# Delta-rule layer of a hybrid decoder trunk: small-tile products of a head pair gathered outside its chunk loop

## Chip, cores and metric

The kernel runs on one core of one Trainium2 chip. The metric is the time of one execution on the device, in microseconds (us); lower is better.

## What is computed

Four decoder layers run one after another over 1024 tokens of 1024 channels: a short gated convolution, a state-space layer, a delta-rule layer (RWKV-7 time mixing), and a second convolution layer. After each mixer come a gated projection and a layer norm. The change lies in the delta-rule layer alone. Per head of 64 channels it keeps a 64 by 64 state and walks over the tokens:

```python
def _rwkv_step(state, inp):
    r_t, w_t, k_t, v_t, kk_t, a_t = inp
    sa = jnp.einsum("bhvk,bhk->bhv", state, -kk_t)
    state = (state * w_t[:, :, None, :] + sa[..., None] * (kk_t * a_t)[:, :, None, :]
             + v_t[..., None] * k_t[:, :, None, :])
    out = jnp.einsum("bhvk,bhk->bhv", state, r_t)
    return state, out
```

The kernel does this by chunks of 64 tokens. Within a chunk the corrections of the tokens depend on each other through a triangular matrix, so a chunk needs the inverse of a unit triangular 64 by 64 matrix; then the state goes from chunk to chunk. Decay w, rate a, keys k, values v, queries r and the gate z come from projections of the shifted input. The outputs are group-normed, get a bonus, and are gated by silu(z).

## The kernel before, in words

The wide projections (`mm3`, lines 299 to 313) take three products of 128 by 128 by 512 per block of 128 input channels, with each operand split in a high and a low part. Their weights are loaded and split ahead by `wload` (line 277).

`rwkv_layer` (line 1289) goes over two halves of 512 tokens. Per half it first computes two low-rank products for decay and rate (`lora`, line 1314): 16 products into one accumulator `pwa` (lines 1329 to 1334), each fed by a freshly built mix. Then come eight blocks of the gate z (`use_z`), which also make the decay and rate of a block out of the low-rank results with a high-part product over 128 rows and a low-part product over 64 rows (lines 1360 to 1365). Then eight blocks of v (`use_v`). Last comes the phase of keys and queries, one head pair (a block m of 128 channels, two heads, eight chunks; pairs are numbered 0 to 7) after another:

- `use_k` (line 1393) makes keys and correction queries. Line 1408 sums squares, line 1419 takes the reciprocal, and lines 1422 to 1427 spread it over the channels with eight products of a broadcast column against the identity (16 passes on TensorE; every product of plain 32-bit numbers in this kernel shows as two passes, a transpose as one). Lines 1436 to 1438 transpose the queries.
- `use_r` (line 1443) makes the queries and the bonus.
- `prep` (line 1649) makes the scores of the pair's chunks (line 1672), copies out the diagonal 32 by 32 blocks, transposes the keys (line 1696), and forms the values' share of the correction (line 1707) with the two halves of the array (chunk parity w) in turns.
- `tsolve` (line 1714) inverts the diagonal blocks on VectorE.
- `join` (line 1747) puts the diagonal inverses together into the inverse T of each 64 by 64 matrix: for each parity w first the products zp (line 1765), a copy, the products tp (line 1770), a copy. Then the corrected queries a2 (line 1781). All these are products of 32 or 64 rows and columns.
- `seq` (line 1788) walks the eight chunks. Per chunk: the state product p1 (line 1801, 128 by 128), the inverse times the values added to it (line 1804, two products of 64 by 64), a copy to `uv` on ScalarE (line 1805), the key product p2 in two halves of 64 columns (line 1809), two updates of the state on VectorE (line 1812), the output products in two halves added to p1 (line 1816), a copy of the output (line 1817). After the loop: group norm, bonus, gate, and a store of the block (lines 1819 to 1850).

The eight banks of PSUM in this layer are three for the wide products (`pmm`), two in `paux` (preparation, join, `use_z`, `use_v`), one in `pk` (`pwa`, and the small products of `use_k` and `use_r`), and two in `pseq`, where p1, p2 and the transpose of the output take turns.

The functions are generators, and `rwkv_layer` (lines 1512 to 1575) pulls them in turns: `seq` of pair m-2 and `tsolve` of pair m-1 beside `use_k` and `use_r` of pair m; then `prep` of pair m, the join of pair m-1, and so on. The steps of `seq` and `tsolve` are issued with a raised priority (`PS, PT = 300, 300`, by `prio`, line 1463); a planner puts the instructions of each engine in a fixed order before the kernel runs, by these priorities and by what depends on what. Each engine then works through its list in that order. A buffer that is asked for again is given in program order, when its earlier tenant has been read.

## Time and profile before

| What | Value |
|---|---|
| median of three runs | 2888.84 us |
| lowest and highest of them | 2883.97 and 2890.22 us |
| span of the profiled execution | 2887.0 us |
| TensorE products, weight loads | 2790.6 us (97%), 2193.9 us (76%) |
| VectorE, ScalarE, GpSimd | 1916.1 us (66%), 1137.6 us (39%), 641.8 us (22%) |

The span runs from the first to the last instruction of one profiled execution. The profiled execution's whole time is not listed apart from the three runs; its span lies between the lowest and the highest of them. PE is TensorE's products, PEld its weight loads, DVE is VectorE, ACT ScalarE, POOL GpSimd. PEclk is the clock that TensorE was granted, as a share of full speed. Busy times of PE are modelled from overlapping products: the distance from one start to the next says more than the duration.

### The profile page before, as it was taken

To read this page: it belongs to the slowest core of one execution; us is meant where nothing else is said; L and a number is where in the kernel's file an instruction comes from. 1 tells how busy PE (TensorE), PEld (TensorE's weight loads), DVE (VectorE), ACT (ScalarE), POOL (GpSimd) and SP (SyncE) were. 2 spreads that over 40 slices of the span, in tenths; PEclk is the share of its full clock that TensorE was granted. 3 is DMA by queue.
4 is the path that set the end of the run, shared out by engine and by line. 5 is a ranking of instruction groups with operands and counts; after the bars stand their busy time and mean duration, and the time that the engine had idled before them with its cause. 6 is when DMAs were issued, how large, how long until landed. Compare 5 with 4: busy or idle time off the path is not lost. (4 is left out here: it accounts for less than half of the span.)

```text
span 2887.0 us, 41522 instructions
## 1 busy us (share of the span) xinstructions
PE 2790.6 (97%) x15515; PEld 2193.9 (76%) x15515; DVE 1916.1 (66%) x3428; ACT 1137.6 (39%) x2229; POOL 641.8 (22%) x689
## 2 busy tenths in 40 slices
PE   8999999999999999999999899999999999999998
PEld 7887788778877887677676577777778778888887
DVE  6777765476657348877987776898757473333654
ACT  3333322232254224665555665565434231112322
POOL 1243413221107043003333102333132210000000
PEclk9999999999999999997998899999899999999999
DMA  5333322267773234452222254222334332112311
GB/s 166 98 96 94 95 75 66 89 177 208 223 243 108 94 100 131 153 181 84 91 76 86 84 174 140 73 80 74 99 105 141 101 88 59 51 44 66 117 65 38
DMA packets 449752, 312.72 MB, mean 108 GB/s; under 512 B 48360, under 2 KB 393744, under 8 KB 449552
## 3 DMA queue, kind: packets, MB, share of 16 engines
q1 hardware_dynamic: 449552, 310.08, 35.6%
q8 instruction: 122, 2.00, 0.3%
q14 instruction: 78, 0.64, 0.1%
HBM read 240.28 MB, written 69.21 MB: 107 GB/s over the span
## 5 line engine op out<-in xcount | busy, mean ns | idle before, releaser
L286 DVE TENSOR_TENSOR wl<-wraw,wh 128x1024 fp32r<-128x1024 f32 x283 | 367.1, 1298 | 305.6 <-ACT wh L285 301.2
L285 ACT CAST wh<-wraw 128x1024 fp32r<-128x1024 f32 x283 | 297.3, 1051 | 687.9 <-PE gp L309 185.6
L1812 DVE SCALAR_TENSOR_TENSOR state<-state,pc,p 64x64 f32<-64x64 f32 x256 | 71.5, 279 | 79.0 <-PE p L1809 70.9
L608 POOL TENSOR_TENSOR ln_s<-ln_s,rp 128x512 f32<-128x512 f32 x42 | 61.5, 1464 | 204.9 <-DVE rp L604 204.9
L1738 DVE TENSOR_TENSOR tv<-ti,mi 128x128 f32<-128x128 f32 (+3 forms) x128 | 91.7, 716 | 3.2 <-PE tp L1770 1.1
L1805 ACT COPY uv<-p 64x128 f32<-64x128 f32 x128 | 33.4, 261 | 126.5 <-PE p L1804 125.2
L308 PE MATMUL zp<-x_0h,wh 128*128 128x512 f32 x192 | 76.8, 400 | 0.0
L310 PE MATMUL gp<-r_0h,wl 128*128 128x512 f32 x192 | 76.4, 398 | 0.0
L308 PE MATMUL gp<-r_1h,wh 128*128 128x512 f32 x192 | 76.3, 398 | 0.0
L310 PE MATMUL gp<-r_1h,wl 128*128 128x512 f32 x192 | 76.2, 397 | 0.2 <-DVE wl L286 0.2
L623 POOL TENSOR_TENSOR rp<-r_0h,r_0l 128x512 f32<-128x512 f32 x24 | 39.9, 1690 | 163.9 <-PE op L309 163.9
L308 PE MATMUL zp<-x_1h,wh 128*128 128x512 f32 x192 | 75.8, 395 | 0.0
L308 PE MATMUL gp<-r_0h,wh 128*128 128x512 f32 x192 | 75.8, 395 | 0.0
L310 PE MATMUL zp<-x_1h,wl 128*128 128x512 f32 x192 | 75.8, 395 | 0.0
L309 PE MATMUL gp<-r_0l,wh 128*128 128x512 f32 x192 | 75.8, 395 | 0.0
L309 PE MATMUL zp<-x_0l,wh 128*128 128x512 f32 x192 | 75.7, 394 | 0.0
L309 PE MATMUL zp<-x_1l,wh 128*128 128x512 f32 x192 | 75.7, 394 | 0.0
L310 PE MATMUL zp<-x_0h,wl 128*128 128x512 f32 x192 | 75.7, 394 | 0.0
L309 PE MATMUL gp<-r_1l,wh 128*128 128x512 f32 x192 | 75.4, 393 | 0.0
L1672 PE MATMUL s<-ra,kb 64*128 64x128 f32 x512 | 71.5, 320 | 1.1 <-DVE ra L1444 1.1
L1816 PEld LDWEIGHTS p<-uv,scr 128*64 128x64 f32 x512 | 43.2, 145 | 37.9 <-ACT uv L1805 22.7
L1801 PEld LDWEIGHTS p<-state,ra 128*128 128x128 f32 x256 | 46.3, 205 | 29.5 <-issue 7.5
(738 smaller groups left out, 8626.5 us busy)
## 6 DMA issues: line engine op xcount, KB each, us to landing
wraw<-in_conv_w_in_dram SPq DMA_DIRECT2D x80, 512.0 KB
wraw<-in_rwkv_w_rkvz_dram SPq DMA_DIRECT2D x64, 512.0 KB
wraw<-in_ple_gate_dram SPq DMA_DIRECT2D x56, 512.0 KB
wraw<-in_conv_w_out_dram SPq DMA_DIRECT2D x24, 512.0 KB
wraw<-in_ssm_w_in_dram SPq DMA_DIRECT2D x21, 512.0 KB
xt<-xd SPq DMA_DIRECT2D x32, 256.0 KB
wraw<-in_rwkv_w_out_dram SPq DMA_DIRECT2D x16, 512.0 KB
wraw<-in_ple_proj_dram SPq DMA_DIRECT2D x14, 512.0 KB
```

Source lines behind the costliest of these rows:

```text
L285: nc.scalar.copy(wh, raw)
L286: nc.vector.tensor_tensor(wl, raw, f32(wh[:]), ALU.subtract)
L308: nc.tensor.matmul(ps, lh, xh, start=(k == 0), stop=False)
L309: nc.tensor.matmul(ps, lh, xl, start=False, stop=False)
L310: nc.tensor.matmul(ps, ll, xh, start=False, stop=(k == kt - 1))
L608: nc.gpsimd.tensor_tensor(s, s, rs, ALU.add)
L623: (eng or nc.gpsimd).tensor_tensor(rs, f32(rh[:]), f32(rl[:]), ALU.add)
L1672: nc.tensor.matmul(pss[hd][:, c * P:(c + 1) * P], kb[rows, 2 * c + w, :], ra[rows, 2 * c + w, :], start=True, stop=True)
L1738: V.tensor_tensor(tv, ti[:, b:8, 4 * b:4 * b + 4].unsqueeze(2).to_broadcast([P, n, c, 4]), mi[:, 4 * b:4 * b + 4, 0:c].rearrange("p q c -> ...
L1801: nc.tensor.matmul(p1[:, 0:P], R.ra[:, c, :], st, start=True, stop=False)
L1812: V.scalar_tensor_tensor(st[cs, cs], st[cs, cs], R.pc[cs, c:c + 1], p2[cs, 0:64], ALU.mult, ALU.add)
L1816: nc.tensor.matmul(p1[rk, cs], R.scr[w][:, c2, hd, :], uv[:, cs], start=False, stop=(hd == 1))
```

## The change

It has these parts. The pool `pk` goes, and its users take buffers from `paux`. `pseq` now has one bank for p2 and the output's transpose, and two for p1: one accumulator per chunk parity that holds four chunks, kept from the join to the end of `seq`. In the join, zp, tp and a2 are made for both parities together, alternating; each accumulator is opened with a product of a two-column zero tile; the products of the inverse with the values, 16 of 64 by 64, go into the accumulators there. In `seq` a chunk has only the state product and one key product of 128 by 128; the output products of all chunks follow in one run after the last key product (`issue_after`), with two copies. In `use_k` the spread of the reciprocal is a broadcast copy on ScalarE and four transposes. The low-part products of decay and rate take 128 rows. `prep` and `join` get a priority of 600. Comments also go from the file. The diff without comment lines, cut:

```diff
-PS, PT = 300,300
+PS, PT, PJ = 300, 300, 600
...
-    S.pk = ls.enter_context(S.tc.tile_pool(name="pk", bufs=1, space=PSUM))
-    S.pseq = ls.enter_context(S.tc.tile_pool(name="pseq", bufs=2, space=PSUM))
+    S.pseq = ls.enter_context(S.tc.tile_pool(name="pseq", bufs=1, space=PSUM))
...
-        pw = pa = S.pk.tile([P, HT], F32, tag="ka", name="pwa")
+        pw = pa = S.paux.tile([P, HT], F32, tag="aux", name="pwa")
...
-        wt = T_("w2", [P, 3, P]).bitcast(F32R)
-        for i, (ps_, rows) in enumerate(((pw, slice(0, 64)), (pa, slice(64, P)))):
+        wt = T_("w2", [P, 4, P]).bitcast(F32R)
+        for i, ps_ in enumerate((pw, pa)):
             raw = w2[i][:, m * P:(m + 1) * P]
             SC.copy(wt[:, i, :], raw)
-            V.tensor_tensor(wt[rows, 2, :], raw[rows], f32(wt[rows, i, :]), ALU.subtract)
+            V.tensor_tensor(wt[:, 2 + i, :], raw, f32(wt[:, i, :]), ALU.subtract)
             nc.tensor.matmul(ps_, wt[:, i, :], L[:, i, :], start=True, stop=False)
-            nc.tensor.matmul(ps_, wt[rows, 2, :], L[rows, i, :], start=False, stop=True)
+            nc.tensor.matmul(ps_, wt[:, 2 + i, :], L[:, i, :], start=False, stop=True)
...
         V.reciprocal(rn, n2)
+        rb = T_("rnb")
+        SC.copy(rb.rearrange("p (g v) -> p g v", v=CH), rn.unsqueeze(2).to_broadcast([P, 8, CH]))
         yield
-        prn = S.pk.tile([P, HT], F32, tag="ka", name="prn")
+        prn = S.paux.tile([P, HT], F32, tag="aux", name="prn")
         for i in range(4):
-            for hd in range(2):
-                q = 2 * i + hd
-                nc.tensor.matmul(prn[hd * 64:hd * 64 + 64, i * P:(i + 1) * P], rn[:, q:q + 1].to_broadcast([P, 64]),
-                                 S.ident, start=True, stop=True)
+            nc.tensor.transpose(prn[:, i * P:(i + 1) * P], rb[:, i * P:(i + 1) * P], S.ident)
...
-                for _ in I.prep(m, h, R):
+                for _ in prio(I.prep(m, h, R), PJ):
...
-                    for _ in I.join(m - 1, h, Rs[m - 1]):
+                    for _ in prio(I.join(m - 1, h, Rs[m - 1]), PJ):
...
+    zero = rg.tile([P, 2], F32, tag="zero", name="zero")
+    G.memset(zero, 0.0)
...
+        R.p1 = [S.pseq.tile([P, 4, P], F32, tag="p1", name="p1", bufs=2) for w in range(2)]
         for w in range(2):
-            rb = rows_b[w]
-            ps = aux("a2")
-            for c2 in range(4):
-                for hd in range(2):
-                    nc.tensor.matmul(ps[hd * 64:hd * 64 + 64, c2 * CH:(c2 + 1) * CH],
+            nc.tensor.matmul(R.p1[w][:, 0, 0:2], S.ident, zero, start=True, stop=False, skip_group_check=True)
+        ps = [aux("a2"), aux("a2")]
+        for c2 in range(4):
+            for hd in range(2):
+                for w in range(2):
+                    rb, cs = rows_b[w], slice(hd * 64, hd * 64 + 64)
+                    nc.tensor.matmul(R.p1[w][rb, c2, cs], tt[rb, 2 * c2 + hd, :], R.uv[w][rb, c2, cs],
+                                     start=False, stop=False, skip_group_check=True)
+        for c2 in range(4):
+            for hd in range(2):
+                for w in range(2):
+                    rb = rows_b[w]
+                    nc.tensor.matmul(ps[w][hd * 64:hd * 64 + 64, c2 * CH:(c2 + 1) * CH],
                                      an[rb, c2, hd * 64:hd * 64 + 64], tt[rb, 2 * c2 + hd, :], start=True, stop=True)
-            SC.copy(r5[:, :, w, acol[w]], ps[:, 0:256].rearrange("p (c t) -> p c t", c=4))
-            yield
+        for w in range(2):
+            SC.copy(r5[:, :, w, acol[w]], ps[w][:, 0:256].rearrange("p (c t) -> p c t", c=4))
...
-            rb, rk = rows_b[w], rows_k[w]
+            rb = rows_b[w]
             uv = R.uv[w][:, c2, :]
-            p1 = sq("p1")
-            nc.tensor.matmul(p1[:, 0:P], R.ra[:, c, :], st, start=True, stop=False)
+            p1 = R.p1[w][:, c2, :]
+            nc.tensor.matmul(p1, R.ra[:, c, :], st, start=False, stop=False, skip_group_check=True)
+            SC.copy(uv[rb, :], p1[rb, :])
+            yield
+            p2 = sq("p2")
+            last = nc.tensor.matmul(p2[:, 0:P], R.kbt[c // 4][:, c % 4, :], uv, start=True, stop=True)
             for hd in range(2):
                 cs = slice(hd * 64, hd * 64 + 64)
-                nc.tensor.matmul(p1[rb, cs], R.tt[rb, 2 * c2 + hd, :], uv[rb, cs], start=False, stop=(hd == 1))
-            SC.copy(uv[rb, :], p1[rb, 0:P])
-            p2 = sq("p2")
-            for hd in (1 - w, w):
-                cs = slice(hd * 64, hd * 64 + 64)
-                nc.tensor.matmul(p2[cs, 0:64], R.kbt[c // 4][:, c % 4, cs], uv[:, cs], start=True, stop=True)
-            for hd in range(2):
-                cs = slice(hd * 64, hd * 64 + 64)
-                V.scalar_tensor_tensor(st[cs, cs], st[cs, cs], R.pc[cs, c:c + 1], p2[cs, 0:64], ALU.mult, ALU.add)
+                V.scalar_tensor_tensor(st[cs, cs], st[cs, cs], R.pc[cs, c:c + 1], p2[cs, cs], ALU.mult, ALU.add)
             yield
-            for hd in range(2):
-                cs = slice(hd * 64, hd * 64 + 64)
-                nc.tensor.matmul(p1[rk, cs], R.scr[w][:, c2, hd, :], uv[:, cs], start=False, stop=(hd == 1))
-            SC.copy(o4[rk, c2, :], p1[rk, 0:P])
-            yield
+        with S.tc.issue_after(last.ins):
+            for c2 in range(4):
+                for hd in range(2):
+                    for w in range(2):
+                        cs = slice(hd * 64, hd * 64 + 64)
+                        nc.tensor.matmul(R.p1[w][rows_k[w], c2, cs], R.scr[w][:, c2, hd, :], R.uv[w][:, c2, cs],
+                                         start=False, stop=True, skip_group_check=True)
+        for w in range(2):
+            SC.copy(o4[rows_k[w]], R.p1[w][rows_k[w]])
```

In the join, zp and tp themselves are the products of before, with `for e in range(8)` now outside `for w in range(2)` and two `aux` tiles at a time.

## Rows read from the trace of the kernel before

**Rows 1.** The page, part 1: busy time, share of the span and instructions.

```profile
PE 2790.6 (97%) x15515; PEld 2193.9 (76%) x15515; DVE 1916.1 (66%) x3428; ACT 1137.6 (39%) x2229; POOL 641.8 (22%) x689
```

**Rows 2.** Stretches: start:end length, busy us (instructions) by engine, PEclk, DMA share, GB/s.

```profile
1331.20:1372.00 40.80, 39.01 (x310) 29.52 (x309) 30.43 (x65) 19.03 (x50) 9.84 (x10) 0.75 0.12 40
...
1853.00:1891.40 38.40, 36.51 (x355) 27.34 (x354) 35.24 (x77) 21.82 (x65) 14.55 (x14) 1.00 0.26 82
...
sum 421.90, PE 398.15 PEld 298.74 DVE 364.46 ACT 232.97 POOL 144.33; mean PE 39.81 PEld 29.87 DVE 36.45 ACT 23.30 POOL 14.43
...
1290.00:2135.00 845.00, 796.82 (x6384) 593.48 (x6384) 667.45 (x1391) 469.64 (x1224) 229.64 (x230) 0.92 0.31 96
...
1546.80:1650.00 103.20, 92.02 (x705) 63.48 (x705) 76.92 (x169) 61.12 (x153) 22.38 (x23) 0.81 0.22 64
...
2018.00:2135.00 117.00, 112.70 (x884) 83.84 (x885) 73.86 (x180) 52.83 (x161) 19.89 (x20) 0.88 0.31 99
```

**Rows 3.** Timeline of TensorE, a chunk of pair 1, second half: start, us, line.

```profile
1873.69 0.40 PE L310 MATMUL sp<-xs1h,wl 128*128 128x512 f32 x1
1873.93 0.39 PE L1801 MATMUL p<-state,ra 128*128 128x128 f32 x2
1874.24 0.44 PE L1804 MATMUL p<-uv,tt 64*64 64x64 f32 x4
1874.62 0.49 PE L308 MATMUL sp<-xs1h,wh 128*128 128x512 f32 x1
1874.95 0.40 PE L309 MATMUL sp<-xs1l,wh 128*128 128x512 f32 x1
1875.27 0.39 PE L1816 MATMUL p<-uv,scr 128*64 128x64 f32 x3
...
1875.76 1.16 PE L1672 MATMUL s<-ra,kb 64*128 64x128 f32 x8
```

**Rows 4.** Timeline of TensorE: runs of small products and transposes of one kind.

```profile
1347.07 1.20 PE L1781 MATMUL a<-tt,ant 64*64 64x64 f32 x30
...
1510.20 1.97 PE L1426 MATMUL prn<-ident,rn 128*64 128x128 f32 x16
...
1514.79 0.66 PE L1438 MATMUL antp<-ident,aq 128*128 128x128 f32 x4
1515.20 0.47 PE L310 MATMUL sp<-xs0h,wl 128*128 128x512 f32 x1
...
2006.77 1.57 PE L1707 MATMUL wps<-uv,sca 64*64 64x64 f32 x32
```

**Rows 5.** Timeline, all engines: a chunk of pair 6 with few wide products about.

```profile
1630.08 0.46 PE L1801 MATMUL p<-state,ra 128*128 128x128 f32 x2
...
1630.94 0.26 ACT L1805 COPY uv<-p 64x128 f32<-64x128 f32 x1 [1.62 <-PE p L1804]
...
1632.74 0.46 PE L1801 MATMUL p<-state,ra 128*128 128x128 f32 x2
```

**Rows 6.** VectorE's waits, 1331.2 to 1546.8, then 1811.7 to 2018: total, times, longest.

```profile
DVE state L1812 <- PE p L1809: 13.2, 16, 2.9
...
DVE state L1812 <- PE p L1809: 13.2, 18, 1.8
```

**Rows 7.** Timeline of TensorE: first and last low-rank products, last of pair 7's join.

```profile
1606.50 1.07 PE L1332 MATMUL pwa<-mix,w 128*64 128x512 f32 x2
...
1635.06 0.59 PE L1334 MATMUL pwa<-mix,w 128*64 128x512 f32 x1
...
1646.90 0.37 PE L1781 MATMUL a<-tt,ant 64*64 64x64 f32 x2
```

**Rows 8.** Groups by line and form, TensorE: low-rank product; busy us, mean ns, idle before.

```profile
L1332 PE MATMUL pwa<-mix,w 128*64 128x512 f32 x32 | 16.9, 609 | 0.0
```

**Rows 9.** Timeline of TensorE: wide products at the lower clock.

```profile
1362.62 0.63 PE L308 MATMUL sp<-xs1h,wh 128*128 128x512 f32 x1
1363.05 0.63 PE L309 MATMUL sp<-xs1l,wh 128*128 128x512 f32 x1
```

More of the change, by code (lines that the diff above doesn't have):

```diff
@@ L1570, in rwkv_layer @@
                 pull(inner)
-            for _ in I.join(NB - 1, h, Rs[NB - 1]):
+            for _ in prio(I.join(NB - 1, h, Rs[NB - 1]), PJ):
                 pass
@@ new lines, in join @@
+        for w in range(2):
+            SC.copy(zs[q1[w]].rearrange("p h c -> p (h c)"), ps[w][q1[w], 0:256])
+        yield
+        ps = [aux("tp"), aux("tp")]
+        for e in range(8):
+            for w in range(2):
+                nc.tensor.matmul(ps[w][q0[w], e * 32:(e + 1) * 32], zs[q1[w], e, :], tt[q1[w], e, 32:64],
+                                 start=True, stop=True)
+        for w in range(2):
+            SC.copy(tt[q0[w], :, 32:64], ps[w][q0[w], 0:256].rearrange("p (h c) -> p h c", h=8))
```

31 lines of the change are left out of this document (16 added, 15 removed).

## The prediction, made before the change was run

> **What bounds the kernel now.** I read the page's busy times first, then the stretches of the one layer that the change touches, then single chunks in the timeline. TensorE is busy for 97% of the span and no other engine for more than 66% [rows 1], so a shorter TensorE list should shorten the kernel, as far as the next engine allows. The delta-rule layer's affected part is the 845 us from 1290 to 2135 us [rows 2]: TensorE 796.82 us, VectorE 667.45 us. Inside it lie ten steady stretches, each from one head pair's norm products to the next pair's (five per half of the tokens, 421.90 us together). There TensorE is busy for 398.15 us, and VectorE for 364.46 us [rows 2]. That is the main reading: VectorE has 57.4 us free in 421.90 us, so whatever TensorE saves beyond that cannot show in these stretches. The two ends of the halves differ: 2018 to 2135 us has TensorE 112.70 of 117.00 us and VectorE only 73.86; 1546.8 to 1650 us has holes on both [rows 2].
>
> The chunk in the timeline shows what TensorE spends [rows 3]. Between whole-array products of 512 columns that follow each other every 0.23 us (1873.69 to 1873.93), a chunk puts two passes of the state product (0.31 us), four passes of 64 rows and columns (0.38 us), and later eight passes of 64 columns (0.49 us). The wide product after the first group takes 0.33 us to its successor, and the one ahead of the second group 0.32 us. Each change between tile shapes thus costs some 0.10 us over the 0.23.
>
> **The change, part by part.** *Chunk loop.* Old cost: 0.31 + 0.38 + 0.10 in the first group, 0.10 + 0.49 + 0.10 around the second, 1.48 us [rows 3]. New: two products of 128 by 128 by 128, four passes. Transposes of that size run four in 0.41 us, start to start [rows 4]; I take 0.42. Upper bound: 2 x 0.31 = 0.62, the present pair with its drain. Saved: 1.06 us a chunk, 8.5 us for the eight chunks of a pair and half (bounds 6.9 and 8.5).
>
> *What comes back outside the loop.* The solve-times-values products become 32 passes in the join. A run of 32 such passes with the array halves in turns took 1.57 us [rows 4], so +1.6. The outputs are 32 passes of 64 columns: at 0.49 / 8 = 0.061 us [rows 3] +2.0; at the 0.040 us of the 64 by 64 run [rows 4] it would be 1.3. I take 2.0. The two zeroing products are four passes, +0.4 at 0.10. The join's older passes (32 x zp, 32 x tp, 32 x a2) now alternate array halves. The alternating run costs 1.57 / 32 = 0.049 us a pass, the one that stays in a half 1.20 / 30 = 0.040 [rows 4]: 96 x 0.009 = +0.9 (bounds 0 and +1.8).
>
> The Trainium skill ("TensorE: Matmul & The Clock Gate", Part 3, The mechanism) says that a weight load overlaps a product in flight only where their row groups differ. By it the alternating run should be the cheaper one, the 0.9 would be nought or a gain, and the sum below would come to 38 us instead of 37. The trace disagrees, 0.049 against 0.040 us.
>
> *Norm spread.* Sixteen passes in 1.97 us give way to four transposes in 0.41 us [rows 4]: -1.5. The spreading copy goes to ScalarE, at most four times the 0.26 us that a copy of 128 columns takes [rows 5]; it is busy for 232.97 of 421.90 us [rows 2], and of the output copies eight small ones become two larger ones. I cost it at nothing. If ScalarE were late, the transposes wait and the key scaling on VectorE behind them.
>
> *Sum on TensorE per pair and half:* -8.5 + 1.6 + 2.0 + 0.4 + 0.9 - 1.5 = -5.1 us; sixteen of them are 82 us. *Low-part products of the decay and rate* go from 64 to 128 rows: two fewer drains in and out for each of 16 blocks, 16 x 4 x 0.10 = 6 us.
>
> *What of it reaches the end.* In the ten steady stretches TensorE would need 398 - 51 = 347 us, less than VectorE's 364. VectorE becomes the bound. Its own list is unchanged: both state updates per chunk, the diagonal solve, the weights' low parts all remain. What can shrink is its waiting. The state update waited 13.2 and 13.2 us for the key product in the two halves [rows 6]. The loop's chain gets shorter: in a chunk with nothing else in the way the period is 2.66 us (1630.08 to 1632.74), the copy of the corrected values starts 0.86 us after the state product [rows 5]. Without the four small passes that copy can start about 0.4 us earlier, and with two passes instead of eight the second group ends about 0.3 us earlier: 2.0 us. I take 25 us off 57 (nothing to 50 are the bounds): most of the 26 us of waits. The join too makes one round of zp and tp with copies instead of two, which helps the same waits.
>
> The first pair of each half only gains the norm spread, two stretches: 3 us. In 2018 to 2135 TensorE is full and output-projection products stand ready: two pairs x 5.1, of which I take 8. In 1546.8 to 1650 the chain of chunks shows: 8 x 0.7, of which 4. The low-part products lie where TensorE and VectorE are both busy: 3 of 6.
>
> *A wait added.* The one-bank pool goes, and its users join the pool of two banks that serves the pair preparation and the join. Most are short tenants in program order. The one that is not is the accumulator of the two low-rank products, which collects 16 products beside their mixes. At the second half it now starts at 1606.50 and ends at 1635.06, ahead of the last join's products at 1646.90 [rows 7]. In the shared pool it comes after that join, so the fill that stood beside the chunk loop of pair 6 moves beside that of pair 7, and the first decay block behind it. Its passes sum to 16.9 us over both halves on one of its two lines [rows 8], the other being its equal in count and shape, so 17 us a half if none overlapped. Bounds 0 and 17; I take -6, since pair 7's chunk loop can use it as fill as pair 6's did. The persistent accumulators (two banks) are given back by a pair's last copies; the next pair's join asks for them after about 5 us of its own zp and tp work, which covers two copies. Queued behind such a wait on TensorE would be wide products planned later.
>
> Sum: 25 + 3 + 8 + 4 + 3 - 6 = 37 us. The profiled execution's span is 2887.0; its own total is not listed apart from the three runs, 2883.97 to 2890.22, with the median 2888.84 only 1.84 above the span. I take the sum off the median: 2852 us.
>
> **Rivals.** *All of TensorE's saving shows* (VectorE's free time can be used up because its waits are all for TensorE): 50 + 3 + 10 + 6 + 6 = 75 us, 2814. For it: nearly every VectorE wait names a TensorE product [rows 6]. Against: that needs a VectorE without holes.
>
> *Nothing shows.* VectorE's list is in fixed order, the waits move to other places, steady stretches give 0, and the shared accumulator costs its whole 17: 3 + 8 + 4 + 3 - 17 = +1 gained, 2888. For it: VectorE at 364 of 422 us already [rows 2].
>
> *Slower: the clock.* TensorE's granted clock is 0.92 over the 845 us [rows 2], so 16% of that time, 135 us, was at 1.2 GHz, the other level being 2.4. At the lower level wide products come every 0.43 us (1362.62 to 1363.05) instead of 0.23 [rows 9]. The stretch from 1331.2 to 1372 had a mean of 0.75 [rows 2], and has a run of a2 passes at 1347.07 [rows 4]. The change gathers small passes into longer runs in every join (128 of them together), and gives TensorE more idle time. If all ten steady stretches fell to 0.75, the 34.7 us that a pair needs would take 46.3 instead of 42.2 now: +41, less the 12 gained elsewhere, +29: 2918. It decides below a clock of about 0.80 there, where 34.7 / 0.80 is 43.4 and eats the other 12; above 0.88 it costs nothing. Against: the stretch from 1853 to 1891.4 holds a join with the same passes, and kept 1.00 [rows 2].
>
> That the change does not do what it says: the instruction order is planned ahead, and the plan may still slip wide products between the small ones. Three more breaks in each of two runs, 0.2 us each, are 1.2 us a pair, 19 us on TensorE, and mostly under VectorE's bound: inside my forecast's own range.
>
> **Chances.** Forecast, 2835 to 2873: 0.45. All of it: 0.15. A weaker gain, 2873 to 2883: 0.07. Nothing: 0.17, of which 0.13 falls within 0.2%, 0.02 to either side. Clock: 0.16. A measurement of this kernel tells 0.2%, 5.8 us, from no change. Faster: 0.45 + 0.15 + 0.07 + 0.02 = 0.69; same 0.13; slower 0.18. The likeliest cases have 2835 to 2873 as their own range; the stated one runs from 2812, the whole saving, to 2902, half way into the clock case, and leaves out about one in ten above and a little below.
>
> **What would show it.** In the changed profile the chunk products should lie at 0.21 us each without a longer wide product beside them; TensorE's busy time from 1290 on should fall by some 50 to 80 us, VectorE's stay near 667. A pair's period should be 38 to 40 us with VectorE's share above 90%. The accumulator of the low-rank products should come after the last join of the first half. I am wrong if the state update's waits stay, if the mean clock of the layer drops under 0.85, or if TensorE waits for ScalarE copies of the join.

## The result: 15 us faster, under half of what was forecast

| Kernel | Median of its runs | Ratio to before, 95% interval | Span | TensorE busy | Span less busy |
|---|---|---|---|---|---|
| before | 2889.53 us (4 runs beside the changed kernel) | 1 | 2887.0 | 2790.6 | 96.4 |
| changed | 2874.39 us (4 runs) | 0.9946 [0.993, 0.9962] | 2873.3 | 2722.6 | 150.7 |

The sign was right; the forecast was 2852. The page of the changed kernel, part 1, answers to [rows 1]:

```profile
PE 2722.6 (95%) x15131; PEld 2163.6 (75%) x15131; DVE 1886.0 (66%) x3428; ACT 1121.9 (39%) x2147; POOL 635.8 (22%) x690
```

TensorE lost 68.0 us of work, and 54.3 us of that came back as time in which it stands still. The stretches say where. Changed kernel: the layer's affected part, a steady pair of the second half, the last of the ten steady stretches (from one pair's norm products to the next), and their sum:

```profile
1290.00:2121.00 831.00, 734.63 (x6029) 564.86 (x6027) 644.98 (x1390) 459.08 (x1148) 235.73 (x235) 0.89 0.32 98
...
1899.40:1936.00 36.60, 33.26 (x341) 24.54 (x340) 32.15 (x76) 21.92 (x62) 13.60 (x14) 1.00 0.28 89
...
1972.60:2016.00 43.40, 35.97 (x292) 30.41 (x292) 30.85 (x76) 21.01 (x60) 14.11 (x13) 0.53 0.20 63
...
sum 384.40, PE 338.11 PEld 264.01 DVE 315.18 ACT 211.09 POOL 132.10; mean PE 33.81 PEld 26.40 DVE 31.52 ACT 21.11 POOL 13.21
```

Against [rows 2], TensorE idles for 96.37 us of this part (831.00 less 734.63), where it was 48.18. In the steady stretches it is at 88% and VectorE at 82%: neither is full. In the changed kernel TensorE waits longest for the state update of the chunk loop (total, times, longest; first the kernel before, then the changed one):

```profile
PE p L1801 <- DVE state L1812: 7.5, 16, 1.4
```

```profile
PE p L1818 <- DVE state L1825: 25.2, 28, 2.8
```

The ten stretches are shorter by 37.5 us in sum, but that is not a gain of the kernel: the norm products moved against the rest of a pair's work, and each half's first stretches, which lie outside the sum, grew. A mark that means the same in both kernels is the first product of a pair's join. Timeline of TensorE, joins of pairs 0, 5 and 7 in each half, kernel before:

```profile
1342.68 0.25 PE L1765 MATMUL zp<-t,m 32*32 32x32 f32 x3
...
1541.41 0.25 PE L1765 MATMUL zp<-t,m 32*32 32x32 f32 x3 [0.86 <-DVE rs_t L1283]
...
1636.63 0.24 PE L1765 MATMUL zp<-t,m 32*32 32x32 f32 x2 [0.19 <-DVE t L1758]
...
1815.09 0.28 PE L1765 MATMUL zp<-t,m 32*32 32x32 f32 x4 [1.17 <-DVE t L1758]
...
2010.49 0.21 PE L1765 MATMUL zp<-t,m 32*32 32x32 f32 x1 [1.03 <-ACT uv L1711]
...
2097.24 0.24 PE L1765 MATMUL zp<-t,m 32*32 32x32 f32 x2
```

The same six marks in the changed kernel:

```profile
1341.86 0.31 PE L1767 MATMUL zp<-t,m 32*32 32x32 f32 x9 [1.82 <-DVE t L1759]
...
1535.51 0.32 PE L1767 MATMUL zp<-t,m 32*32 32x32 f32 x4 [0.36 <-DVE t L1759]
...
1630.20 0.32 PE L1767 MATMUL zp<-t,m 32*32 32x32 f32 x4
...
1815.72 0.25 PE L1767 MATMUL zp<-t,m 32*32 32x32 f32 x5 [1.60 <-DVE t L1759]
...
2008.54 0.26 PE L1767 MATMUL zp<-t,m 32*32 32x32 f32 x2
...
2076.46 0.31 PE L1767 MATMUL zp<-t,m 32*32 32x32 f32 x8
```

Differences of neighbours give the ledger. Pairs 0 to 5 take 193.6 us instead of 198.7, and 192.8 instead of 195.4: 7.7 us gained. Pairs 5 to 7 gain 0.5 in the first half. The border, from the last join of the first half to the first of the second, is 185.5 instead of 178.5: 7.0 lost. Pairs 5 to 7 of the second half gain 18.8 (67.9 instead of 86.8), but the changed kernel is 20.8 us ahead at the last mark and only 13.7 at the end of the span. The 7 between them are one wait: TensorE has done what stands ahead of it in its list and stands still until GpSimd has done its part of the last pair's output. In the kernel before this wait is 1.0 us; in the changed one:

```profile
2124.89 0.69 PE L1860 MATMUL otp<-ident,o 128*128 128x128 f32 x2 [6.79 <-POOL o L1853]
```

In the join, three of the six marks stand behind VectorE's tile of the solve, two before.

The wait that the change was to shorten has shrunk little in the steady stretches. VectorE's waits for the key product, 1349.8 to 1541.1, then 1822.9 to 2016.0 (total, times, longest), answering to [rows 6]:

```profile
DVE state L1825 <- PE p L1822: 10.1, 12, 2.9
...
DVE state L1825 <- PE p L1822: 12.7, 12, 2.0
```

From the first join to the last of each half it fell further, to 15.6 and 14.9 us from 24.3 and 27.8.

### The profile page after: what moved, and what is told of

Same layout as the page of the kernel before. It is cut to its first block, busy times and chain, and to the rows that moved or that the text cites. A ratio compares the mean times of both kernels' runs of the same rounds, so it can differ in the third digit from the quotient of the medians.

```text
span 2873.3 us, 40597 instructions
## 1 busy us (share of the span) xinstructions
PE 2722.6 (95%) x15131; PEld 2163.6 (75%) x15131; DVE 1886.0 (66%) x3428; ACT 1121.9 (39%) x2147; POOL 635.8 (22%) x690
## 4 chain that ended last, share of the span: by engine, by line
PE 73%; DVE 14%; ACT 4%; issue 3%; POOL 2%; DMA 2%; SPq 0%; DVEq 0%; POOLq 0%; ACTq 0%
PE op L309 3%; PE op L308 3%; PE op L310 3%; PE gp L310 3%; PE zp L308 3%; PE gp L309 3%; PE zp L309 3%; PE zp L310 3%; PE gp L308 3%; PE sp L308 3%; PE sp L309 3%; PE sp L310 3%; DVE tv L1739 2%; PE hp L308 2%; PE hp L309 2%
## 5 line engine op out<-in xcount | busy, mean ns | idle before, releaser
L1818 PE MATMUL p<-state,ra 128*128 128x128 f32 x256 | 65.7, 344 | 27.3 <-DVE state L1825 25.2
L1673 PEld LDWEIGHTS s<-ra,kb 64*128 64x128 f32 x512 | 64.2, 212 | 20.4 <-ACT scr L1679 6.5
L1822 PE MATMUL p<-uv,kbt 128*128 128x128 f32 x256 | 67.7, 351 | 10.4 <-ACT uv L1819 10.3
```

The source lines that it names most:

```text
L1673: nc.tensor.matmul(pss[hd][:, c * P:(c + 1) * P], kb[rows, 2 * c + w, :], ra[rows, 2 * c + w, :], start=True, stop=True)
L1818: nc.tensor.matmul(p1, R.ra[:, c, :], st, start=False, stop=False, skip_group_check=True)
L1822: last = nc.tensor.matmul(p2[:, 0:P], R.kbt[c // 4][:, c % 4, :], uv, start=True, stop=True)
```

## Experiments

The expectations were written before each run, with the readings as they stood then. Times are medians; a difference between two kernels is that of their ratios to before, times 2889 us. "Idle" is the span less TensorE's busy time.

| Run | Is | Median | Ratio [95%] | Busy, idle |
|---|---|---|---|---|
| e1_shared_pool | before, `pk` given up | 2903.48 | 1.0059 [1.003, 1.0089] | 2800.8, 104.1 |
| e5_short_tenants | before, only the small users moved | 2904.23 | 1.0049 [1.003, 1.0069] | 2802.3, 94.4 |
| e6_acc_wide | changed, accumulator out of `paux` | 2859.91 | 0.9891 [0.9873, 0.991] | 2715.1, 145.7 |
| e12_two_wide | e2 with `pk` back, two wide banks | 2900.53 | 1.005 [1.0024, 1.0076] | 2754.5, 145.7 |
| e2_prio0 | changed, no raised priority | 2863.39 | 0.9925 [0.9898, 0.9953] | 2736.5, 130.6 |
| e7_acc_wide_prio0 | e6 and e2 together | 2848.4 | 0.9856 [0.9837, 0.9874] | 2721.7, 125.7 |
| e8_before_prio600 | before, raised priority | 2900.13 | 1.0038 [1.0024, 1.0051] | 2781.0, 117.4 |
| e13_prio30 | e7, priority 30 | 2854.08 | 0.989 [0.9865, 0.9915] | 2723.1, 125.8 |
| e14_prio570 | changed, priority 570 | 2872.14 | 0.9942 [0.9922, 0.9961] | 2726.2, 142.8 |
| e9_in_loop | e7, small tiles back in the loop | 2893.79 | 1.001 [0.9995, 1.0025] | 2793.7, 94.3 |
| e15_after_in_loop | changed, small tiles back in the loop | 2943.07 | 1.0197 [1.0171, 1.0223] | 2833.5, 111.6 |
| e10_old_spread | e7, old spread | 2876.56 | 0.9948 [0.993, 0.9966] | 2754.1, 129.1 |
| e16_after_old_spread | changed, old spread | 2865.78 | 0.9929 [0.9905, 0.9954] | 2719.3, 142.7 |
| e11_join_turns | e7, one parity after the other | 2891.14 | 0.9993 [0.9976, 1.0009] | 2766.9, 117.9 |
| e3_wide_more | changed, 30 us more wide products | 2873.74 | 0.9956 [0.9936, 0.9976] | 2732.2, 133.0 |
| e17_wide_more8 | changed, 60 us more | 2893.08 | 1.0017 [0.9994, 1.0039] | 2762.4, 127.6 |
| e18_fast_wide_more | e7, 30 us more | 2901.89 | 1.0052 [1.0033, 1.0071] | 2780.5, 117.6 |
| e4_short_solve | changed, shorter solve on VectorE | 2843.53 | 0.9854 [0.9825, 0.9883] | 2704.5, 137.3 |

### What the shared pool costs

**e1_shared_pool.** The kernel before, with the pool part of the change alone; the bank set free stays unused:

```diff
-    S.pk = ls.enter_context(S.tc.tile_pool(name="pk", bufs=1, space=PSUM))
...
-        pw = pa = S.pk.tile([P, HT], F32, tag="ka", name="pwa")
+        pw = pa = S.paux.tile([P, HT], F32, tag="aux", name="pwa")
...
-        pss = S.pk.tile([P, HT], F32, tag="ka", name="pss")
+        pss = S.paux.tile([P, HT], F32, tag="aux", name="pss")
```

(`prn`, `antp` and `pb` likewise.)

> The kernel before with one part of the change alone: the users of the one-bank pool take buffers from the two-bank pool; the freed bank stays unused. Chain theory (the time is set by the chain from one pair's join to the next and by the chunk chains at the end of each half; TensorE's saving only lets wide products run ahead): between 2 us faster and 8 us slower than before, the low-rank products some 5 us later in the first half and some 30 us later in the second. Pool theory (the shared buffers ate what was missing of the forecast): 15 to 22 us slower than before. Clock theory (TensorE is still the bound, the saving went into a lower granted clock): no difference beyond 5 us.

Measured: 17 us slower. That is the forecast's upper bound for the pool, but that bound was worked out for the accumulator alone, and the next run shows that it is met by chance.

**e5_short_tenants.** The same with `pwa` left in `pk`, so that only `pss`, `prn`, `antp` and `pb` move.

> The kernel before, where the small products of keys and queries take buffers from the two-bank pool, and the accumulator of the low-rank products alone keeps the bank of its own. If the accumulator is what cost the 17 us of the shared pool: within 5 us of before. If the small products are, by waiting for banks that preparation and join hold: 10 to 18 us slower. From the wide products' positions in the run with the whole pool shared (11 us behind from the border of the halves on, 6 more in the second half): some 6 us slower.

Measured: 14 us slower. In the kernel before, most of the 17 are the small products of `use_k` and `use_r`, which I had put down as short tenants that cost nothing. The accumulator adds 3 there, which the intervals of the two runs don't tell from nothing.

**e6_acc_wide.** The changed kernel with the accumulator among the wide products' banks:

```diff
-        pw = pa = S.paux.tile([P, HT], F32, tag="aux", name="pwa")
+        pw = pa = S.pmm.tile([P, HT], F32, tag="mm", name="pwa")
```

> The changed kernel, where the accumulator of the low-rank products takes one of the three banks of the wide products in place of one of the two shared ones. Accumulator theory: 6 to 12 us faster than the changed kernel (the products start again ahead of the last join of the first half, near 1605 us). If the wide products need their third bank there, or the small products are the cost: within 4 us.

Measured: 16 us faster than the changed kernel, more than the 6 to 12 expected. The accumulator's products by source line (count: minimum, median and maximum in ns, first and last start), first in the changed kernel, then in this one:

```profile
L1331 PE MATMUL pwa<-mix,w x32: 592/592/643, 1161.6 to 1647.2; 128*64 128x512 f32 x32
```

```profile
L1331 PE MATMUL pwa<-mix,w x32: 592/640/1115, 1156.0 to 1606.8; 128*64 128x512 f32 x32
```

The second half's products end at 1606.8 instead of 1647.2, as they did before the change (1635.06, [rows 7]) or earlier. That is the border of the halves, and there this term lies: from the last join of the first half to the first of the second it takes 174.0 us (1629.13 to 1803.10), 11.6 less than in the changed kernel, of the 12.5 that the spans differ. The same holds without the raised priority (e2 and e7, below): 199.8 us with the accumulator in `paux`, 180.4 without, and 20 us in time.

**e12_two_wide.** e2 (below) with the bank `pk` given back to all its old users, paid for by the third wide bank:

```diff
-    S.pmm = ls.enter_context(S.tc.tile_pool(name="pmm", bufs=3, space=PSUM))
+    S.pmm = ls.enter_context(S.tc.tile_pool(name="pmm", bufs=2, space=PSUM))
+    S.pk = ls.enter_context(S.tc.tile_pool(name="pk", bufs=1, space=PSUM))
```

> The changed kernel without the raised priority, with the one-bank pool restored for all its users of before and two banks instead of three for the wide products. If the small products' waits for shared banks cost more than the third wide bank is worth: 10 to 20 us faster than the changed kernel without the raised priority (2863 us), so near 2848 us. If the third bank is what lets wide products run ahead beside the chains: slower than 2863 us by 5 us or more.

Measured: 36 us slower than e2. The third wide bank is worth more than `pk`, so this says nothing on what the small tenants cost within the changed kernel. That stays open.

### What the raised priority costs

**e2_prio0**, the changed kernel, and **e7_acc_wide_prio0**, e6, each with

```diff
-PS, PT, PJ = 300, 300, 600
+PS, PT, PJ = 300, 300, 0
```

> The changed kernel with preparation and join at no raised priority (0 in place of 600). Chain theory: 5 to 20 us slower than the changed kernel, as the pair's chain then queues behind wide products and chunk work. If the raised priority itself is what costs (early preparation pushes the chunk loop back in the lists): 5 to 15 us faster. Clock theory: within 5 us, with the lower clock's share as it is.

> The changed kernel with both: the accumulator in a bank of the wide products, and no raised priority of preparation and join. If the two costs are separate, 16 to 24 us faster than the changed kernel, near 2852 us; if both name the same delay at the border of the halves, as fast as the better one of them alone, near 2863 us.

Measured: e2 is 6 us faster than the changed kernel, an interval that overlaps with the changed kernel's; e7 is 10 faster than e6, and 42 faster than before. e7 is the version that beats both kernels. Its layer, the second half's joins 0 to 5, and VectorE's wait for the key product in that stretch:

```profile
1290.00:2095.00 805.00, 734.51 (x6019) 554.69 (x6018) 655.87 (x1388) 462.13 (x1147) 236.84 (x235) 0.93 0.33 101
...
1814.70:1995.50 180.80, 164.85 (x1664) 126.56 (x1663) 165.38 (x376) 109.50 (x304) 68.81 (x69) 0.97 0.28 83
...
DVE state L1825 <- PE p L1822: 3.6, 6, 1.7
```

TensorE is busy for as long as in the changed kernel, to 1 us; what is gone is idle time, 25.0 us. In the second half both engines are at 91%, and the state update waits 3.6 us instead of 12.7; between joins 0 and 5 of the first half it waits 8.2. Its marks of joins 0, 5 and 7:

```profile
1343.38 0.32 PE L1767 MATMUL zp<-t,m 32*32 32x32 f32 x7 [2.54 <-DVE t L1759]
...
1548.72 0.31 PE L1767 MATMUL zp<-t,m 32*32 32x32 f32 x2 [0.48 <-ACT uv L1712]
...
1625.75 0.22 PE L1767 MATMUL zp<-t,m 32*32 32x32 f32 x2
...
1806.12 0.25 PE L1767 MATMUL zp<-t,m 32*32 32x32 f32 x5 [1.35 <-DVE t L1759]
...
1986.94 0.24 PE L1767 MATMUL zp<-t,m 32*32 32x32 f32 x2 [1.65 <-ACT uv L1712]
...
2057.02 0.25 PE L1767 MATMUL zp<-t,m 32*32 32x32 f32 x4
```

The gain is not even: the first half's pairs 0 to 5 take 205.3 us, longer than before (198.7), its pairs 5 to 7 only 77.0 instead of 95.2; the second half's take 180.8 instead of 195.4.

**e8_before_prio600.** The kernel before with the same raise:

```diff
-                for _ in I.prep(m, h, R):
+                for _ in prio(I.prep(m, h, R), 600):
```

(the join likewise.)

> The kernel before with the raised priority of 600 for preparation and join alone. If the priority costs by itself: 5 to 15 us slower than before. If it costs only together with the shared pool or the accumulators kept by a pair: within 5 us of before.

Measured: 11 us slower. So the raise costs some 6 to 11 us with or without the gathered tiles. Why it does, no run shows.

**e13_prio30** (e7 with 30 in place of 0) and **e14_prio570** (the changed kernel with 570 in place of 600) ask whether such differences are an accident of one order.

> The fastest kernel so far (2848 us) with a priority of 30 in place of 0 for preparation and join, which should move next to nothing by itself. If the planned order is steady under such an edit: within 4 us of 2848. If its 2848 us hang on a lucky order: 8 to 25 us slower, and the prices read from undoing single parts on it are too high by as much.

> The changed kernel with a priority of 570 in place of 600 for preparation and join. If the order is steady: within 4 us of the changed kernel (2874). If any edit scatters the order: up to 15 us to either side.

Measured: e13 is 6 us by the medians (10 by the ratios) slower than e7, e14 2 us (1) faster than the changed kernel. An edit that should move nothing moved up to 10 us, so a single cost of that size can be an accident of one order. For the raised priority three pairs of kernels agree in sign (6, 10, 11); e9's 44 us are well above, e6's 16 not by far.

### What the gathering is worth

**e9_in_loop.** e7 with the products of the inverse and the output products in the loop, per chunk, each with its copy; the kept accumulators and the whole key product stay:

```diff
             nc.tensor.matmul(p1, R.ra[:, c, :], st, start=False, stop=False, skip_group_check=True)
+            for hd in range(2):
+                cs = slice(hd * 64, hd * 64 + 64)
+                nc.tensor.matmul(p1[rb, cs], R.tt[rb, 2 * c2 + hd, :], uv[rb, cs], start=False, stop=False,
+                                 skip_group_check=True)
...
+            for hd in range(2):
+                cs = slice(hd * 64, hd * 64 + 64)
+                nc.tensor.matmul(p1[rows_k[w], cs], R.scr[w][:, c2, hd, :], uv[:, cs],
+                                 start=False, stop=True, skip_group_check=True)
+            SC.copy(o4[rows_k[w], c2, :], p1[rows_k[w], :])
```

> The fastest kernel so far (the changed one with the accumulator in a bank of the wide products and no raised priority), with the two groups of small products back in the chunk loop: the inverse times the values ahead of each copy, the outputs after each key product, with an output copy a chunk. The kept accumulators and the whole-array key product stay. Chain theory: TensorE's work in the loop matters only through the chunk chains at the ends of the halves and through VectorE's waits: 5 to 18 us slower than that kernel. If gathering them is the whole gain: 35 to 45 us slower, back at the time of before.

Measured: 44 us slower than e7, the time of before. Page and one steady pair:

```profile
PE 2793.7 (97%) x15131; PEld 2210.9 (77%) x15131; DVE 1907.4 (66%) x3428; ACT 1145.7 (40%) x2245; POOL 634.3 (22%) x690
...
1393.20:1429.80 36.60, 36.52 (x334) 27.61 (x332) 32.05 (x82) 23.53 (x67) 12.94 (x15) 1.00 0.24 74
```

With the tiles in the loop TensorE is full, 36.52 of 36.60 us, and has 72 us more to do at the same number of products.

**e15_after_in_loop.** The same on the changed kernel, but with one step of the generator a chunk: the edit also takes out the `yield` behind the copy to `uv`, so the expectation's "two steps" does not hold. The kernel before, the changed one and e9 have two.

> The changed kernel itself with the two groups of small products back in the chunk loop (two steps a chunk for the generator, as before the change). If gathering is worth what it was on the fastest version: 35 to 45 us slower than the changed kernel, TensorE at 97% or more of the steady stretches. If the shared accumulator and the priority hide it: 10 to 25 us slower.

Measured: some 70 us slower than the changed kernel, more than either case of the expectation. `seq` is pulled by steps, so with one step a chunk it is issued at another pace beside the wide products, and the 70 us are no price of the gathering alone. A steady pair of it:

```profile
1436.20:1479.70 43.50, 43.26 (x346) 33.71 (x345) 31.96 (x76) 23.54 (x67) 13.45 (x15) 0.89 0.23 75
```

Full again. That the gathering takes work off TensorE is shown by e9; e15 agrees in that.

**e10_old_spread** and **e16_after_old_spread**: e7 and the changed kernel with the sixteen-pass spread in place of the copy and four transposes.

```diff
-        rb = T_("rnb")
-        SC.copy(rb.rearrange("p (g v) -> p g v", v=CH), rn.unsqueeze(2).to_broadcast([P, 8, CH]))
...
-            nc.tensor.transpose(prn[:, i * P:(i + 1) * P], rb[:, i * P:(i + 1) * P], S.ident)
+            for hd in range(2):
+                q = 2 * i + hd
+                nc.tensor.matmul(prn[hd * 64:hd * 64 + 64, i * P:(i + 1) * P], rn[:, q:q + 1].to_broadcast([P, 64]),
+                                 S.ident, start=True, stop=True)
```

> The same fastest kernel with the old spread of the reciprocal: eight small products against the identity in place of a ScalarE copy and four transposes. TensorE gets 1.5 us more per pair and half, 24 us in all. Chain theory: within 5 us of that kernel, either way, as the copy on ScalarE leaves the chain too. If TensorE's work shows: 10 to 24 us slower.

> The changed kernel itself with the old spread of the reciprocal by eight small products. If the 27 us of the same edit on the fastest version were its own price: 20 to 30 us slower than the changed kernel. If they were mostly scatter of the order: within 8 us.

Measured: on e7 the old spread costs 27 us, close to the 24 us of work that it adds (16 x 1.5). On the changed kernel it costs nothing; the 5 us that it gains are inside the intervals. I read this as a price that shows where TensorE's work sets the time and not where it doesn't. That is not shown: the order's scatter of up to 10 us is in both numbers, and the clock differs too (below).

**e11_join_turns.** e7 with zp and tp of one parity after the other, as before the change.

```diff
-        ps = [aux("zp"), aux("zp")]
-        for e in range(8):
-            for w in range(2):
-                nc.tensor.matmul(ps[w][q1[w], e * 32:(e + 1) * 32], R.m10[q0[w], e, :], t1[q0[w], e, :],
+            ps = aux("zp")
+            for e in range(8):
+                nc.tensor.matmul(ps[q1[w], e * 32:(e + 1) * 32], R.m10[q0[w], e, :], t1[q0[w], e, :],
```

> The same fastest kernel with zp and tp of the join one array half after the other again, each with its copy, as before the change. This adds two copies' round trips to the chain of a pair, some 2.5 us, and with the alternating runs gone some 0.8 us of TensorE. Chain theory: 15 to 40 us slower (16 joins, about 2.5 us each at most). If the chain through the join is covered by other waits: within 5 us.

Measured: 40 us slower than e7, the upper end of the expectation. The affected part of the layer:

```profile
1290.00:2135.00 845.00, 780.14 (x6011) 599.66 (x6010) 659.59 (x1381) 458.49 (x1139) 230.69 (x233) 0.88 0.31 96
```

TensorE's busy time rose by 45 us on the page, more than the passes themselves account for (64 passes a pair and half at 0.016 us, below, are 1.0, times 16 is 16 us). The mean clock is 0.88 where e7 has 0.93. Which of clock and order came first this run cannot say.

### What bounds the changed kernel

**e3_wide_more**, **e17_wide_more8** (changed kernel) and **e18_fast_wide_more** (e7): the first product of each wide product of keys and queries is issued 4, 8 and 4 times more. Its result is overwritten, so nothing of the computation changes. By 16 pairs and halves, two wide products and 0.23 us this is 30, 60 and 30 us of TensorE's time.

```diff
+        for _ in range(more if k == 0 else 0):
+            nc.tensor.matmul(ps, lh, xh, start=True, stop=True)
...
-    k_mm = lambda m, h: mm3(S, wprep(S, "rwkv_w_rkvz", (0, 1), m * P), xs[(1, h)], "sp")
+    k_mm = lambda m, h: mm3(S, wprep(S, "rwkv_w_rkvz", (0, 1), m * P), xs[(1, h)], "sp", more=4)
```

> The changed kernel, where each wide product of keys and queries issues its first product four more times (each starts the sum anew, so nothing of the result changes): 32 x 4 more products of 512 columns, at 0.23 us some 30 us more work for TensorE, none of it in the chain of a pair. Chain theory: 0 to 10 us slower than the changed kernel. Clock theory with TensorE as the bound: 20 to 30 us slower, or less if the denser work keeps the clock, in which case the time at the lower clock in the layer falls from 188 us to under 140.

> The changed kernel with eight more first products in each wide product of keys and queries: 256 more, some 60 us of TensorE's work at full clock, 30 more than in the run with four. Chain theory: TensorE still has slack (it idled for 82 of 820 us with four more), so under 15 us slower than the changed kernel. Clock theory (TensorE is the bound, what it saved went into the lower clock): 20 to 35 us slower than the run with four, unless the time at the lower clock falls by another 50 us, to some 90.

> The fastest version (accumulator in a bank of the wide products, no raised priority; 2848 us) with the 128 more wide products, some 30 us of work. Chain theory: at most 10 us slower than it. Clock theory: 20 to 30 us slower, as there is little lower clock left there to win back (116 us in the layer).

Measured: 30 us of work added to the changed kernel cost nothing (0.9956 against 0.9946), 60 cost 20 (more than the 15 of the chain reading, and 18 over e3, just under the 20 of the clock reading), and 30 added to e7 cost 54 by the medians, more than either reading had. The affected part of the layer in the three, in this order:

```profile
1290.00:2110.00 820.00, 738.08 (x6130) 564.42 (x6128) 650.53 (x1379) 456.58 (x1142) 234.77 (x233) 0.92 0.32 99
```

```profile
1290.00:2135.00 845.00, 771.08 (x6258) 590.53 (x6256) 660.46 (x1381) 457.55 (x1144) 229.75 (x232) 0.93 0.31 97
```

```profile
1290.00:2149.00 859.00, 792.77 (x6142) 601.61 (x6141) 670.48 (x1396) 459.48 (x1147) 232.52 (x238) 0.90 0.31 95
```

The mean clock moved when work was added, and not in one direction. Of the levels 1.2 and 2.4 GHz the mean tells the time at the lower one, 2 x (1 - mean) x length; as the mean is given to 0.01, such a time is good to some 8 us. That is 183 us in the changed kernel (0.89), 131 and 118 in e3 and e17, but 172 in e18 against 113 in e7. At the lower level a wide product takes 0.43 us instead of 0.23 [rows 9], so a microsecond there does about half the work. By that e3 has up to 26 us given back, which hides its 30, and e18 loses up to another 30 beside its 30. So these runs leave two readings of the changed kernel: TensorE has slack and the chain of a pair sets the time, or added work raised its clock. By e17, 60 less 33 given back is 27, near the 20 measured, which speaks for the second.

**e4_short_solve.** The changed kernel without the three row steps of the diagonal solve in `tsolve`: that part of the inverse is left out, TensorE's list is untouched.

```diff
-        for q in range(3):
+        for q in range(0):
```

> The changed kernel without the first three row steps of the diagonal solve (it leaves out the part that makes rows of a group of four independent, so the inverse lacks those terms): 12 VectorE instructions less per pair and half, some 8 to 9 us of VectorE. Chain theory: the interval from one pair's join to the next falls by 4 to 8 us, the whole by 25 us or more. Clock theory: under 10 us faster, since TensorE has the same work.

Measured: 2843.53, 27 us (31 by the medians) faster than the changed kernel. Page:

```profile
PE 2704.5 (95%) x15131; PEld 2146.4 (76%) x15131; DVE 1824.8 (64%) x3236; ACT 1122.8 (40%) x2147; POOL 632.3 (22%) x690
```

VectorE lost 61.2 us of work (3.8 a pair and half, where the expectation had 8 to 9), and half of it shows in the time although VectorE is at 82% in the steady stretches. That is the size which the chain reading named: the end is set by the chain from one join to the next, with the solve as a link. But from join to join a pair takes only 3.5 us less in the first half and 0.5 in the second, not 4 to 8, and the clock rose here too. The affected part of the layer in e4, then in e16:

```profile
1290.00:2090.00 800.00, 714.51 (x6020) 546.66 (x6018) 582.72 (x1200) 457.81 (x1145) 231.04 (x235) 0.92 0.33 102
```

```profile
1290.00:2110.00 820.00, 730.72 (x6205) 560.33 (x6205) 643.77 (x1387) 447.53 (x1126) 237.13 (x234) 0.91 0.32 99
```

By the same arithmetic e4 has 128 us at the lower level and up to 27 given back, as much as its whole gain, and e16 148 and up to 17 of its 24. So neither run separates the two readings. For the chain speak TensorE's waits for the state update, 25.2 us in the changed kernel, 7.5 before and 14.3 in e7; and that from the changed kernel to e7 the time at the lower level falls by 70 us, but TensorE's busy time in this part by 0.12 us. How the 183 us at the lower level split into cause and consequence of the standing still stays open.

## Why the forecast was right in sign and wrong in size

**Where TensorE's saving comes from: right, with mis-sized terms.** A chunk, timeline of TensorE in the changed kernel:

```profile
1880.71 1.14 PE L1708 MATMUL wps<-uv,sca 64*64 64x64 f32 x16
1881.78 0.49 PE L1818 MATMUL p<-state,ra 128*128 128x128 f32 x2
...
1883.04 0.40 PE L309 MATMUL sp<-xs1l,wh 128*128 128x512 f32 x1
1883.27 0.38 PE L1822 MATMUL p<-uv,kbt 128*128 128x128 f32 x2
1883.41 0.48 PE L310 MATMUL sp<-xs1h,wl 128*128 128x512 f32 x1
1883.73 0.40 PE L308 MATMUL sp<-xs1h,wh 128*128 128x512 f32 x1
...
1885.98 0.49 PE L1822 MATMUL p<-uv,kbt 128*128 128x128 f32 x2
1886.23 0.48 PE L310 MATMUL sp<-xs1h,wl 128*128 128x512 f32 x1
1886.54 0.39 PE L308 MATMUL sp<-xs0h,wh 128*128 128x512 f32 x1
```

Two passes take 0.14 to 0.25 us, and the wide product behind them 0.31 or 0.32 instead of 0.23. I had named "without a longer wide product beside them" as the sign: it is there. Two such products cost 0.46 (both as at 1883.27) to 0.66 us (both as at 1885.98), not the 0.42 forecast. So the 0.10 that I had put down to a change of tile shape comes, as 0.08, without one too. The end of the loop and the join of the next pair, same view:

```profile
1890.42 1.15 PE L1832 MATMUL p<-uv,scr 128*64 128x64 f32 x32
1891.50 0.50 PE L310 MATMUL sp<-xs0h,wl 128*128 128x512 f32 x1
...
1894.89 0.78 PE L1775 MATMUL tp<-tt,t 32*32 32x32 f32 x32
1895.60 0.50 PE L308 MATMUL sp<-xs0h,wh 128*128 128x512 f32 x1
...
1896.49 1.09 PE L1791 MATMUL p<-uv,tt 64*64 64x64 f32 x29
...
1897.47 0.69 PE L1797 MATMUL a<-tt,ant 64*64 64x64 f32 x28
1898.09 0.50 PE L308 MATMUL sp<-xs0h,wh 128*128 128x512 f32 x1
```

The outputs take 1.08 / 32 = 0.034 us a pass, not 0.061. The alternating runs, which I held dearer, are cheaper: tp 0.71 / 32 = 0.022 us a pass, T times uv with a2 1.60 / 64 = 0.025. Runs that stay in a half took 0.040 for a2 [rows 4] and 0.038 for tp in the kernel before, 0.61 us from this row to the a2 run at 1347.07 [rows 4]:

```profile
1346.46 0.69 PE L1770 MATMUL tp<-tt,t 32*32 32x32 f32 x16
```

The row I priced them from, the wps run [rows 4], was not alike: it alternates too, and stays dear after the change, 1.07 / 16 = 0.067 us a pass (1880.71 to 1881.78). The Trainium skill ("TensorE: Matmul & The Clock Gate", Part 3, The mechanism) has weight loads pulled ahead of products in flight where the row groups don't conflict, by which the alternating runs would be the cheaper ones. The join after the change agrees (0.022 to 0.025 against 0.038 to 0.040), the wps run does not; my "the trace disagrees" held for the one row that I had. In sum the misses favour the change: chunk -8 x (1.48 - 0.56) = -7.4 at the middle of the two, outputs +1.1, the join's 128 passes 64 x 0.022 + 64 x 0.025 - 64 x 0.038 - 32 x 0.040 = -0.7, zero +0.4, spread -1.5: -8.1 us a pair and half instead of -5.1. By this TensorE's busy time should have fallen by 130; from 1290 on it fell by 62.2, inside the 50 to 80 that I named (VectorE's, which was to stay, fell by 22.5). The lower clock may take up to 24 of the difference (183 us at the lower level instead of 135); the rest I can't place.

**"What of it reaches the end", 25 us in the steady stretches: this step failed in its size.** Measured, it is 7.7 between the joins. I had taken VectorE's busy time, 364 of 422 us, as the next bound; "VectorE becomes the bound" is not borne out, 82% instead of over 90. The state update's waits, most of which were to go, are 10.1 and 12.7 us instead of 13.2 and 13.2. This was my own sign of being wrong. Of the other two, the mean clock of the layer is 0.89, not under 0.85, and TensorE waits 2.0 us in the layer for the join's copy of a2, no more. A pair's period is 38.6 us by the joins, inside the 38 to 40 that I named, but by that mark it was 39.4 before. Why the stretches give no more, by the chain or by the clock, stays open (e3 to e18).

**"A wait added", -6: this step failed.** The accumulator alone costs 16 us in the changed kernel (e6) and 20 without the raised priority (e2 against e7), around the upper bound of 17 that I had worked out and set aside because pair 7's chunk loop could take the fill. It came after the first half's last join, as forecast, but what stood behind it, the second half's first blocks, came later too: the border takes 185.5 us, 178.5 before and 174.0 in e6. The same step put the small products down as short tenants at nothing. On the kernel before they cost 14 (e5); within the changed kernel their cost stays open.

**The raised priority: never priced.** It is in the diff, and costs 6 (e2) to 10 us (e7 against e6; e8 says 11). Accumulator and priority are 26 us together. Without them the change is worth 42, and the forecast's 37 plus the 6 taken off for the accumulator is 43. So in sum the missing 22 us are what these two cost. That the sums meet so well is luck, as the places show. Gains by the marks, in us of span:

| Place | Forecast | Changed | e7 |
|---|---|---|---|
| up to join 0 (first pairs of both halves in the forecast) | 3 | 0.8 | -0.7 |
| joins 0 to 5, both halves | 25 | 7.7 | 8.0 |
| joins 5 to 7, first half | 4 | 0.5 | 18.2 |
| border (wait added, low-part products) | -6 + 3 | -7.1 | -1.9 |
| from join 5 of the second half on | 8 | 11.8 | 16.0 |
| sum | 37 | 13.7 | 39.6 |

In e7 too the steady stretches give 8.0 of the 25, and the ends give 34 where I had 12. Wide products move from one place to another, so a place tells where time was saved, not by what. Nor do the runs tell how accumulator and priority cost it, by the waits alone or through the clock: without them the time at the lower level falls from 183 to 113 us, which is up to 35 us of TensorE's work.

**The ends.** Second half: 18.8 gained between joins 5 and 7, some 12 after the last pair's output, against 8. First half: 0.5 against 4. A lead of the wide products that can't be kept is part of it: counting the wide products with a low-part weight in order of start, those of the same number come up to 64 us earlier than before the change (at about 2030 us of the kernel before), and only 14 earlier at 2180. In the first half the lead is 55 us at 1515 and gone at 1666. I read it so: they are done while chain work is about, and the last pairs then have nothing to stand beside them, as in the wait of 6.79 us at 2124.89.

**The rivals.** "Nothing shows" gave 2888 with the pool at its whole 17, near what the accumulator costs here. "The clock" wanted a mean below 0.80 in the steady stretches. Their mean is 0.89, with four of the ten at 1.00 and the last at 0.53, so it did not turn the sign. But my "above 0.88 it costs nothing" was too good: 183 us at the lower level instead of 135 are up to 24 us. And the rival's sum was too dear: it divides by 0.75 a time of 34.7 us that was itself taken at a mean of 0.95. Two parts were never undone alone: the low-part products over 128 rows (forecast: 3), and the accumulators kept by a pair with one bank left for p2.

## What to carry to other kernels

Gathering small tiles out of a loop of whole-array products pays where TensorE is full, 44 us here (e9); but price each buffer that is given up for it by all its tenants, by who stands in line behind the longest of them at a border between stages, and on the kernel that it goes into: the same accumulator cost some 3 us in the kernel before and 16 in the changed one. A change of priorities in the same diff is a change of its own: price it, or run it alone. When busy time falls and the span doesn't follow, write down span less busy for each kernel: it tells at once whether work came back (e9: 72 us) or standing still did (here: 54 us).

## What the hardware showed that I had not expected

- Passes of 32 by 32 in turns on the two halves of the array take 0.022 us each, and 0.038 in one half; the wps run, in turns too, takes 0.049 [rows 4] to 0.067.
- A wide product behind a whole-array 32-bit product takes 0.31 us instead of 0.23, with no change of tile shape (1883.41 to 1883.73). In the kernel before the same stood behind a run of transposes, 1515.20 [rows 4].
- 30 us of added wide products went with a rise of the layer's mean clock from 0.89 to 0.92 and cost nothing in the changed kernel; in e7 the same products went with a fall from 0.93 to 0.90 and cost 54 us.
